# Two transformer half-layers on one Trainium2 core: the last two pairs of gate and up go to down's places without DRAM, the modulation sums are spread over the stages, one input combination moves to Pool

## The chip, the cores and the metric

The kernel runs on one core of a Trainium2 chip. The metric is the device time in microseconds of one execution; the time before is the median of three executions. Engines are named as in the profile: PE (matmul), DVE (vector), ACT (scalar), POOL (GpSimd), SP (the engine whose queue issues nearly all DMAs here).

## The reference

A hybrid decoder layer on x of 1024 tokens by 1024 columns, all float32, cut to what matters here:

```python
mod = (silu(c) @ w_ada + b_ada).reshape(9, 1024)          # nine modulation vectors
h = rms_norm(x, norm_ffn1) * (1 + mod[1]) + mod[0]
x = x + 0.5 * mod[2] * ((silu(h @ ffn1_gate) * (h @ ffn1_up)) @ ffn1_down)   # D_FF = 2816
h = rms_norm(x, norm_mix) * (1 + mod[4]) + mod[3]
...                                                        # projections, gated DeltaNet heads, pooling heads
x = x + mod[5] * (mixed @ w_out)
h = rms_norm(x, norm_ffn2) * (1 + mod[7]) + mod[6]
x = x + 0.5 * mod[8] * ((silu(h @ ffn2_gate) * (h @ ffn2_up)) @ ffn2_down)
return rms_norm(x, final_norm)
```

## The kernel before

**Precision.** Every float32 operand is split into a high part (ACT copy to fp32r) and a low part (DVE: value minus high part), and a product of a 128x128 weight block with a 128x512 activation tile is three matmuls of 512 columns: high by high, high by low, low by high.

**The two FFNs.** D_FF is cut into 22 columns of 128, in 11 pairs. Each of the two halves (`st` 0 and 1, for ffn1 and ffn2) computes one pair of gate and up directly, and the other ten as 2x2 block products with seven multiplications instead of eight (`SLOTS`: p1, p2, p5, p6, p3, p7, q4). Each slot needs a weight block or a sum of weight blocks, split into high and low (`split_weights`), and an input or a combination of inputs, also split (`combine_task`, `combo_split`). The combinations are made before the first pair of seven, from the four normed quarters `XN`. The seven products of a weight pair are added up while they are read out of PSUM (`gate_read`, `up_read`), and `parts_task` makes from the four results of a pair the seven parts that the down product takes as input, some by subtractions on POOL. Then ten of the pairs go through down in sevens again (`seven`, kind "d": thirteen products of 1, 2, 3, 4, 4, ... pairs of depth), and the last pair directly (`last_pair`).

**Ring.** The split parts of all pairs are written to DRAM (`part_task`, tensors gd) and come back into four places (pair modulo 4) of the tiles H, G, U and zs (`ring_task`, tiles H<-gd, G<-gd). These places are the very tiles that hold the inputs of gate and up, so for the first four pairs each of the seven kinds becomes free only with its last use in the last gate/up pair (flag `vfree`); for later pairs, when down has used the pair four before (`gfree`). The sums of down are added onto the residual rows, which come back from DRAM too (`rest_task`, A<-xpark in the first half, A<-rest in the second); they take their tiles from the sixteen A tiles that gate and up use as temporaries.

**Modulation vectors.** Two of the nine (scale and shift of the first norm) are made at the start. The other seven are made by `ada_tasks`, in fourteen chunks of 512 columns: eight DMAs of 256 KB into `ad` tiles, eight DVE instructions that add the weighted rows, four PE transposes into an `aux` bank, a DVE reduction.

**Order.** A planner (class `Order`) runs generators with assumed durations (`yield ("V", 0.6)` and so on: V is DVE, S is ACT, G is POOL, D is the DMA queue) and ranks, and the instructions of PE, DVE and ACT stay in the order in which it emits them. So an instruction whose input is late holds all that stand behind it on its engine. All DMAs of this part are issued on SP's one queue, in order as well; an SP instruction whose tile is not free holds the rest.

Of the kernel before, what the change touches and what calls it, by code (L numbers as in the profile page):

```python
# [11 lines left out]
ALU = mybir.AluOpType  # L12
# [12 lines left out]
NS = NPAIR - 1  # L25

# [110 lines left out]
def hybrid_layer_kernel(  # L137
# [367 lines left out]
    def w0_loads(u):  # L505
        return {(f, m): unit_load(w.rearrange("a (k p) f -> p (a k) f", p=P)[:, 4 * u : 4 * u + 4, f * P : (f + 1) * P]) for f, m, w in first}
# [117 lines left out]
    up1 = wunit(wsrc(ffn1_up, 1)[0])  # L624
# [80 lines left out]
    def ada_load(j, ch, k, cell):  # L705
        yield ("D", 0.5)
# [14 lines left out]
    def ada_tasks():  # L721
# [3 lines left out]
        for j, ch in seq:  # L725
            for k in range(KT):
                yield flag("ad", j, ch, k)
                raw, acc = cells[j, ch, k][0], cells[j, ch]
                yield ("V", 0.66 if k else 0.4)
# [50 lines left out]
    for st in range(2):  # L780
        wg, wu, wd = gates[st]
        todo = []
        for j in range(1, NPAIR):
# [33 lines left out]
    def seven_raws(st):  # L817
        for n, e in enumerate(plans[st]):
            tag = "cv" if n % 2 else "raw"
            for b in ("11", "21", "22", "12"):  # L820
                yield need(tag)
                yield ("D", 0.5)
# [7 lines left out]
    def seven_splits(st):  # L830
        for n, v in slots:
            yield need("split")
            spawn(split_weights(st, n, v), 1 if n < 2 else 3)

    def split_weights(st, n, v):
        nk = plans[st][n]["nk"]
        tt, cp = 0.08 + 0.13 * nk, 0.1 + 0.105 * nk
# [86 lines left out]
    def gate_read(st, n, v, ps, banks):  # L924
        j = plans[st][n]["j"]
        key = {"p2": (0, 0), "p3": (0, 1), "q4": (1, 0), "p7": (1, 1)}
        if v in ("p1", "p5", "p6"):
            yield need("tmp")
            yield ("S", 0.52)
# [4 lines left out]
        if v == "q4":  # L934
            yield need("tmp")
            yield ("S", 0.52, "Silu")
# [3 lines left out]
        else:  # L940
# [3 lines left out]
            yield ("V", 0.6)  # L944
# [5 lines left out]
            yield ("S", 0.52, "Silu")  # L950
# [4 lines left out]
    def up_read(st, n, v, ps, banks):  # L955
        j = plans[st][n]["j"]
        key = {"p2": (0, 0), "p3": (0, 1), "q4": (1, 0), "p7": (1, 1)}
        if v in ("p1", "p5", "p6"):
            yield need("tmp")
            yield ("S", 0.52)  # L960
# [4 lines left out]
        if v == "q4":  # L965
            yield flag("silu", st, j, key[v])
            i, t = made["s", st, j, key[v]]
            yield ("V", 0.6)
            V.tensor_tensor(t, t, ps, op=ALU.mult)
            put("mm")  # L970
        else:
# [3 lines left out]
            yield ("V", 0.6)  # L975
# [7 lines left out]
            yield ("V", 0.6)  # L983
# [5 lines left out]
    def down_read(st, n, v, ps, banks):  # L989
# [5 lines left out]
        yield ("V", 0.66)  # L995
# [11 lines left out]
    def silu_task(st, j, f, h, ps, tag):  # L1007
        yield need("tmp")
        yield ("S", 0.52, "Silu")
# [5 lines left out]
    def glu_task(st, j, f, h, ps, tag):  # L1015
        yield flag("silu", st, j, (f, h))
        yield ("V", 0.6)
# [8 lines left out]
    def first_rest():  # L1026
# [9 lines left out]
        spawn(glu_task(0, 0, 1, 1, ps, "mm"), 0.8)  # L1036

    def combine_task(st):
# [9 lines left out]
        for i, v in enumerate(("p5", "p7", "p6", "q4")):  # L1048
            for k in range(KT // 2):
                xa, xb, xc, xd = XN[k, 0], XN[k, 1], XN[k + 4, 0], XN[k + 4, 1]  # L1050
                b = shift[:, k + 4 : k + 5]
                yield ("V", 0.62)
                if i == 0:
                    V.tensor_tensor(xa, xb, xa, op=ALU.subtract)
                elif i == 1:
                    V.scalar_tensor_tensor(xb, xd, db[:, k : k + 1], xb, op0=ALU.add, op1=ALU.subtract)
                elif i == 2:
                    V.scalar_tensor_tensor(xd, xd, b, xa, op0=ALU.add, op1=ALU.subtract)
                else:
# [960 lines left out]
```

## Time and profile before

| | us |
|---|---|
| median of three runs | 1903.33 (1902.78 to 1908.27) |
| the profiled execution | 1904.2 |
| its span, first to last instruction | 1902.4 |
| PE busy in the span | 1806.9 |
| DVE busy in the span | 1395.1 |
| ACT busy, POOL busy | 773.3, 281.2 |

The profiled execution is 0.9 us over the median and has 1.8 us outside its span. Busy time of PE counts a matmul at either clock level as busy, so a stage can be busy and still slower than another. By stage: start and first products to about 97 us; gate and up of ffn1 to 529; down of ffn1 to about 735; projections, heads and output to about 1251; ffn2 the same again to about 1830; the last pair and the final norm to the end.

### The profile page before, as it was taken

What the parts mean: (1) busy time and instruction counts of PE and PEld (TensorE: products, weight loads), DVE (VectorE), ACT (ScalarE), POOL (GpSimd) and SP (SyncE); (2) the same over time, 40 slices, a digit from 0 to 9 for tenths busy, and PEclk for the clock granted to TensorE, in tenths of its full rate; (3) what the DMA queues carried; (4) which work ended last, traced back from release to release, by engine and by line L of the source; (5) the groups of instructions that cost most, each with busy time, mean ns of one, the idle gap of its engine ahead of it and who ended that gap; (6) DMA issues with size and microseconds to landing.
All of it is one profiled execution on the core that took longest, in us unless ns stands there. A gap on an engine that the chain in (4) does not pass through costs nothing.

```text
span 1902.4 us, 24995 instructions
## 1 busy us (share of the span) xinstructions
PE 1806.9 (95%) x8437; PEld 1483.4 (78%) x8437; DVE 1395.1 (73%) x2450; ACT 773.3 (41%) x1527; POOL 281.2 (15%) x229
## 2 busy tenths in 40 slices
PE   7899898999979999999999999999999999979997
PEld 6677776788858887788888878878888888758876
DVE  4899999886666667878787674696667666756676
ACT  5453333344422223464344253354444444312225
POOL 3421111111100003121121012211211121000004
PEclk9889999999989999999999999999999999989998
DMA  9447777755698754122121135415345535997722
GB/s 329 160 128 244 237 232 227 235 192 181 231 348 275 248 176 140 45 63 49 34 48 47 46 124 154 122 62 193 122 137 180 170 122 166 330 331 257 232 79 89
DMA packets 311008, 322.66 MB, mean 170 GB/s; under 512 B 28437, under 2 KB 215890, under 8 KB 310880
## 3 DMA queue, kind: packets, MB, share of 16 engines
q1 hardware_dynamic: 310304, 319.93, 52.3%
q8 instruction: 67, 1.10, 0.2%
q0 software_dynamic: 576, 1.13, 0.2%
q14 instruction: 61, 0.50, 0.1%
HBM read 223.21 MB, written 97.78 MB: 169 GB/s over the span
## 4 chain that ended last, share of the span: by engine, by line
PE 76%; DVE 11%; DMA 7%; issue 3%; ACT 1%; POOL 1%; SPq 0%; ACTq 0%; POOLq 0%; DVEq 0%
PE mm L155 44%; PE po L155 24%; PE aux L155 7%; DVE A L155 3%; DVE ad L155 2%; DVE split L155 2%; PE rec L155 2%; DVE pm L155 1%; DMA ad<-in_w_ada 1%; DMA gd<-A 1%; DMA adah<-in_w_ada 1%; DMA G<-gd 1%; DVE G L155 1%; DMA H<-gd 1%; DMA raw<-in_ffn_gate 1%
## 5 line engine op out<-in xcount | busy, mean ns | idle before, releaser
L155 PE MATMUL mm<-H,split 128*128 128x512 f32 (+1 forms) x3096 | 770.2, 396 | 8.8 <-DVE A L155 7.2
L155 PEld LDWEIGHTS mm<-H,split 128*128 128x128 f32 x3096 | 571.3, 190 | 126.7 <-DVE A L155 7.4
L155 PE MATMUL po<-H,split 128*128 128x512 f32 x1584 | 390.1, 395 | 32.4 <-DVE A L155 25.8
L155 PEld LDWEIGHTS po<-H,split 128*128 128x128 f32 x1584 | 298.8, 190 | 99.9 <-issue 28.3
L155 PE MATMUL mm<-G,split 128*128 128x512 f32 x1440 | 348.9, 394 | 2.5 <-DVE G L155 1.8
L155 PEld LDWEIGHTS mm<-G,split 128*128 128x128 f32 x1440 | 272.6, 190 | 62.6 <-DVE G L155 3.2
L155 ACT CAST split<-pm 128x512 fp32r<-128x512 f32 (+3 forms) x264 | 152.8, 581 | 352.7 <-DVE pm L155 351.5
L155 DVE TENSOR_TENSOR split<-pm,split 128x512 fp32r<-128x512 f32 (+3 forms) x264 | 185.0, 704 | 108.7 <-ACT split L155 105.5
L155 POOL TENSOR_TENSOR A<-A,A 128x512 f32<-128x512 f32 x80 | 125.2, 1574 | 666.7 <-DVE A L155 420.4
L155 ACT CAST split<-raw 128x512 fp32r<-128x512 f32 (+2 forms) x199 | 117.2, 595 | 187.2 <-PE mm L155 107.8
L155 PE MATMUL po<-U,split 128*128 128x512 f32 x480 | 156.7, 392 | 4.1 <-DVE A L155 4.1
L155 DVE TENSOR_TENSOR split<-raw,split 128x512 fp32r<-128x512 f32 (+2 forms) x199 | 133.2, 679 | 19.2 <-ACT split L155 18.9
L155 DVE SCALAR_TENSOR_TENSOR A<-mm,fg,A 128x512 f32<-128x512 f32 (+1 forms) x144 | 103.1, 718 | 54.9 <-PE mm L155 36.8
L155 DVE TENSOR_TENSOR A<-A,A 128x512 fp32r<-128x512 f32 (+1 forms) x208 | 141.1, 691 | 2.2 <-ACT A L155 2.2
L155 PEld LDWEIGHTS po<-U,split 128*128 128x128 f32 x480 | 90.7, 189 | 24.1 <-ACT A L155 2.6
L155 POOL TENSOR_TENSOR acc<-acc,cv 128x512 f32<-128x512 f32 (+1 forms) x46 | 56.6, 1229 | 345.0 <-ACT cv L155 343.9
L155 DVE SCALAR_TENSOR_TENSOR A<-po,fg,A 128x512 f32<-128x512 f32 x78 | 58.1, 749 | 53.9 <-PE po L155 44.0
L155 PE MATMUL po<-zs,split 128*128 128x512 f32 x240 | 94.1, 392 | 0.0
L155 ACT CAST split<-cv 128x512 fp32r<-128x512 f32 (+1 forms) x96 | 57.0, 594 | 90.8 <-PE po L155 52.2
L155 DVE SCALAR_TENSOR_TENSOR ad<-ad,cs,ad 128x512 f32<-128x512 f32 x98 | 84.5, 863 | 11.9 <-DMA ad<-in_w_ada 10.8
L155 ACT CAST A<-A 128x512 fp32r<-128x512 f32 x148 | 88.5, 619 | 10.3 <-DVE A L155 8.4
L155 DVE TENSOR_TENSOR split<-cv,split 128x512 fp32r<-128x512 f32 (+1 forms) x96 | 64.1, 668 | 21.9 <-ACT split L155 21.4
(270 smaller groups left out, 1821.1 us busy)
## 6 DMA issues: line engine op xcount, KB each, us to landing
gd<-A SPq DMA_DIRECT2D x296, 256.0 KB, 3.9
H<-gd SPq DMA_DIRECT2D x88, 512.0 KB, 4.6
ad<-in_w_ada SPq DMA_DIRECT2D x112, 256.0 KB, 3.3
raw<-in_ffn_gate SPq DMA_DIRECT2D x88, 256.0 KB, 3.8
cv<-in_ffn_up SPq DMA_DIRECT2D x80, 256.0 KB, 4.5
G<-gd SPq DMA_DIRECT2D x80, 256.0 KB, 3.7
raw<-in_w_in SPq DMA_DIRECT2D x40, 256.0 KB, 2.9
adah<-in_w_ada SPq DMA_DIRECT2D x32, 256.0 KB, 5.9
```

What stands on the lines that cost most here:

```text
L155: ins = f(*args, **kwargs)
```

## The change

- The direct pair is now pair 1 (`PAIR0`), and the ten others come in the order 3 to 10, then 0, then 2 (`PAIRS`). The last two (`DIRECT`) skip `part_task` and DRAM: `direct_task` writes high and low part right into the place that down reads, when `vfree` of the slot has come. Pairs 1 and 3, the other two of the first four places, are read back from DRAM, and their writes have been issued long before. `ring_task` and `rest_task` become `feed_task` and `rest_load`.
- The fourteen chunks of the modulation vectors start at flags (`start`): those of mod 2, 4 and 3 from the weights of the third pair of ffn1 on, mod 5 and 7 in down of ffn1, mod 6 in the projections, mod 8 in ffn2. In the built program six of the fourteen stand ahead of down of ffn1, four in it, two in the projections, two in ffn2; before, all fourteen stood ahead of down of ffn1.
- Of the four combinations of the inputs, the third (p7) is a POOL subtraction without the shift (`combine_third`); the shift goes into the high and low part.
- H tiles are loaded from DRAM by two DMAs of 256 KB instead of one of 512 KB, and the planner's assumed durations are larger (DVE 0.6 to 0.7, a DMA 0.5 to 0.78, and so on).

```diff
+PAIR0 = 1
+PAIRS = (3, 4, 5, 6, 7, 8, 9, 10, 0, 2)
+DIRECT = PAIRS[-2:]
...
     def ada_loads(seq, cells):
+        start = {(2, 0): ("W", 0, 4, "p1"), (5, 0): ("gfree", 0, 0, "q4"), (6, 0): ("H", 1, KT - 1, 1), (8, 0): ("W", 1, 4, "p1")}
         for j, ch in seq:
+            if (j, ch) in start:
+                yield flag(*start[j, ch])
             yield need("ad")
...
-        for j in range(1, NPAIR):
+        for j in PAIRS:
...
-        for i, v in enumerate(("p5", "p7", "p6", "q4")):
...
+        for k in range(KT // 2):
+            yield ("V", 0.72)
+            V.tensor_tensor(XN[k, 0], XN[k, 1], XN[k, 0], op=ALU.subtract)
+            spawn(combo_split(st, k, "p5", XN[k, 0]), 1.4)
+            spawn(combine_third(st, k, db[:, k : k + 1]), 1.5)
...
+    def combine_third(st, k, b):
+        yield ("G", 1.3)
+        G.tensor_tensor(XN[k, 1], XN[k + 4, 1], XN[k, 1], op=ALU.subtract)
+        mark(("t3", st, k))
+        spawn(combo_split(st, k, "p7", XN[k, 1], b), 1.4)
...
         for v, src in todo:
+            if j in DIRECT:
+                spawn(direct_task(st, j, v, *src), 1.6 if j == DIRECT[0] else 2.8)
+                continue
...
+    def direct_task(st, j, v, i, src):
+
+        yield flag("vfree", st, v)
+        yield ("S", 0.62)
+        mv = ring[st, j, v] = place_of(v, j)
+        S.copy(mv[0], src)
+        yield ("V", 0.7)
+        V.tensor_tensor(mv[1], src, mv[0].bitcast(F32), op=ALU.subtract)
+        release(i)
+        mark(("G", st, j, v))
...
-    def ring_task(st):
+    def feed_task(st):
 
         for p in range(NPAIR):
             r = p % 4
+            if p < 4:
+                for d in (2 * p, 2 * p + 1):
+                    for h in range(2):
+                        spawn(rest_load(st, d, h), 2.5)
+            if p in DIRECT:
+                continue
             for v in SLOTS if p < NS else ((0, 0), (0, 1), (1, 0), (1, 1)):
```

**DVE in the third of the ten pairs of ffn1.** The order on DVE of the kernel before, around its reads of the slots p7 (ad is a sum of a modulation chunk, split and pm are weights, an A on both sides is a product being read out or a part):

```order
L155 SCALAR_TENSOR_TENSOR ad_427_1929<-ad_462_2082,cs_157,ad_427_1929 128x512
L155 TENSOR_TENSOR A13_432_1949<-A13_432_1949,mm_394_1794 128x512
L155 SCALAR_TENSOR_TENSOR ad_427_1929<-ad_464_2093,cs_157,ad_427_1929 128x512
L155 TENSOR_TENSOR split_469_2128<-raw_451_2037,split_469_2128 128x512
L155 SCALAR_TENSOR_TENSOR ad_427_1929<-ad_465_2097,cs_157,ad_427_1929 128x512
L155 TENSOR_TENSOR A12_440_1980<-A12_440_1980,mm_400_1820 128x512
L155 SCALAR_TENSOR_TENSOR ad_427_1929<-ad_466_2106,cs_157,ad_427_1929 128x512
L155 TENSOR_TENSOR A12_440_1980<-A12_440_1980,A13_432_1949 128x512
L155 TENSOR_TENSOR split_472_2151<-cv_463_2086,split_472_2151 128x512
L155 SCALAR_TENSOR_TENSOR ad_427_1929<-ad_468_2115,cs_157,ad_427_1929 128x512
```

The changed kernel around the same two reads (the helper's line is 160 there):

```order
L160 TENSOR_TENSOR split_434_2011<-cv_428_1979,split_434_2011 128x512
L160 TENSOR_TENSOR A9_405_1869<-A9_405_1869,mm_370_1721 128x512
L160 TENSOR_TENSOR split_436_2027<-raw_425_1963,split_436_2027 128x512
L160 SCALAR_TENSOR_TENSOR ad_371_1726<-ad_419_1931,cs_157,ad_371_1726 128x512
L160 TENSOR_TENSOR A14_412_1898<-A14_412_1898,mm_375_1744 128x512
L160 SCALAR_TENSOR_TENSOR ad_371_1726<-ad_423_1953,cs_157,ad_371_1726 128x512
L160 TENSOR_TENSOR A14_412_1898<-A14_412_1898,A9_405_1869 128x512
L160 TENSOR_TENSOR split_439_2052<-cv_435_2022,split_439_2052 128x512
L160 TENSOR_TENSOR pm_443_2075<-raw_408_1879,raw_411_1896 128x512
L160 SCALAR_TENSOR_TENSOR ad_371_1726<-ad_437_2036,cs_157,ad_371_1726 128x512
```

The sums of modulation chunks stand thinner: of their 112 first-step and adding instructions 3 stood in the first of the ten pairs, 18 to 20 in each of the second to sixth, 13 in the seventh; now 4 stand in the second pair, 12, 13 and 12 in the next three, 7 in the sixth.

**SP where gate and up of ffn1 end.** The queue before, some way into the loads behind the last gate/up product (H, G, U and zs are places of the ring, gd on the left a part that is written out, A<-xpark a residual row):

```order
L1127 DMA gd_1071_4997<-A8_1023_4827 128x512
L1154 DMA H2_1_1073_5010<-gd_452_2040 128x1024
L1127 DMA gd_1071_4997<-A14_989_4669 128x512
L1154 DMA H3_0_1075_5021<-gd_507_2307 128x1024
L1171 DMA A1_1078_5027<-xpark_180_811 128x512
L1154 DMA H7_0_1081_5037<-gd_510_2316 128x1024
L825 DMA raw_1083_5044<-in_ffn1_down 128x4x128
L1149 DMA U_1085_5050<-gd_516_2346 128x512
L1151 DMA zs_1086_5051<-gd_516_2346 128x512
L1171 DMA A14_1090_5065<-xpark_177_805 128x512
L1149 DMA G6_1092_5073<-gd_520_2361 128x512
L1171 DMA A8_1094_5076<-xpark_181_813 128x512
```

The changed kernel, from the load for slot p1 of pairs 1 and 3 on:

```order
L1197 DMA H1_0_848_4197<-gd_239_1088 128x512 x2
L1197 DMA H3_0_921_4523<-gd_319_1461 128x512 x2
L1197 DMA H5_0_863_4254<-gd_261_1176 128x512
L833 DMA raw_865_4263<-in_ffn1_down 128x128
L1197 DMA H5_0_863_4254<-gd_261_1176 128x512
L1197 DMA H7_0_924_4537<-gd_322_1471 128x512 x2
L1208 DMA A7_867_4278<-xpark_134_593 128x512
L1197 DMA zs_878_4312<-gd_269_1206 128x512
L833 DMA raw_872_4297<-in_ffn1_down 128x128
L833 DMA raw_874_4303<-in_ffn1_down 128x128
L1197 DMA U_877_4311<-gd_269_1206 128x512
L833 DMA cv_890_4366<-in_ffn1_down 128x2x128
```

Before, the loads of three whole pairs, the writes of the last parts and the residual rows stand behind the last gate/up product in one queue; now the loads of pairs 1 and 3 go side by side from slot p1 on, no write stands between them, and pairs 0 and 2 are not in the queue.

**DVE in the third of down's products.** The rows of the kernel before around the first read of the third product (mm_1068, columns 4 and 5):

```order
L155 TENSOR_TENSOR A14_989_4669<-A14_989_4669,A8_1023_4827 128x512
L155 SCALAR_TENSOR_TENSOR A11_1005_4753<-mm_1035_4871,fg0_173,A11_1005_4753 128x512
L155 TENSOR_TENSOR split_1072_4999<-pm_1067_4988,split_1072_4999 128x384
L155 TENSOR_TENSOR pm_1074_5014<-pm_1067_4988,raw_1014_4796 128x384
L155 SCALAR_TENSOR_TENSOR A15_1011_4780<-mm_1068_4990,fg0_173,A15_1011_4780 128x512
L155 TENSOR_TENSOR pm_1079_5031<-raw_1036_4875,pm_1074_5014 128x384
L155 TENSOR_TENSOR split_1076_5023<-pm_1074_5014,split_1076_5023 128x384
```

The changed kernel around the same read (mm_968):

```order
L160 TENSOR_TENSOR split_972_4701<-pm_971_4698,split_972_4701 128x384
L160 TENSOR_TENSOR H2_0_939_4579<-A9_854_4205,H2_0_939_4579 128x512
L160 TENSOR_TENSOR split_974_4706<-pm_973_4703,split_974_4706 128x384
L160 TENSOR_TENSOR H6_0_941_4590<-A6_910_4480,H6_0_941_4590 128x512
L160 TENSOR_TENSOR zs_943_4597<-A13_918_4514,U_942_4596 128x512
L160 SCALAR_TENSOR_TENSOR A0_936_4573<-mm_968_4685,fg0_173,A0_936_4573 128x512
L160 SCALAR_TENSOR_TENSOR A15_905_4461<-mm_933_4567,fg0_173,A15_905_4461 128x512
```

The low parts of pair 2 (H2_0, H6_0, zs) now stand right ahead of that read, which needs the first of them; 33 instructions stand from the first read of down to this one before, 39 now.

## Rows read from the trace of the kernel before

**Rows 1.** The page, busy time by engine: busy us (share of the span) xinstructions.

```profile
PE 1806.9 (95%) x8437; PEld 1483.4 (78%) x8437; DVE 1395.1 (73%) x2450; ACT 773.3 (41%) x1527; POOL 281.2 (15%) x229
```

**Rows 2.** Windows: stretch, its us, busy by engine, clock, DMA share, GB/s.

```profile
96.70:529.20 432.50, 405.04 (x1737) 328.67 (x1736) 372.98 (x569) 183.02 (x324) 65.39 (x39) 0.96 0.66 214
404.00:529.00 125.00, 124.74 (x553) 103.40 (x554) 84.42 (x133) 54.81 (x98) 17.29 (x12) 1.00 0.57 190
529.20:593.60 64.40, 51.34 (x212) 40.23 (x211) 42.82 (x76) 15.83 (x32) 0.00 (x0) 0.89 0.97 333
593.60:735.00 141.40, 141.14 (x622) 116.30 (x620) 91.76 (x151) 31.42 (x58) 1.21 (x2) 1.00 0.60 191
```

**Rows 3.** Timeline of PE, ffn1's gate and up: start us, us, instructions.

```profile
91.22 11.04 PE L155 MATMUL mm<-H,split 128*128 128x512 f32 x48
...
139.06 8.32 PE L155 MATMUL mm<-H,split 128*128 128x512 f32 x36
...
485.69 11.04 PE L155 MATMUL mm<-H,split 128*128 128x512 f32 x48
...
523.77 6.28 PE L155 MATMUL mm<-H,split 128*128 128x512 f32 x27
```

**Rows 4.** Waits of PE in 160:400: us in total, times, longest.

```profile
PE aux L155 <- DVE ad L155: 15.1, 7, 4.2
```

**Rows 5.** Timeline of PE around transposes of modulation chunks.

```profile
176.12 0.66 PE L155 MATMUL aux<-ident,ad 128*128 128x128 f32 x4
176.53 5.26 PE L155 MATMUL mm<-G,split 128*128 128x512 f32 x22
...
271.83 3.33 PE L155 MATMUL mm<-G,split 128*128 128x512 f32 x7
```

**Rows 6.** Groups of instructions, DVE in 160:400: busy us, mean ns.

```profile
L155 DVE SCALAR_TENSOR_TENSOR ad<-ad,cs,ad 128x512 f32<-128x512 f32 x89 | 76.8, 863 | 11.0 <-DMA ad<-in_w_ada 10.1
L155 DVE TENSOR_REDUCE red<-aux 128x4 f32<-128x512 f32 x12 | 8.2, 685 | 1.2 <-PE aux L155 1.1
```

**Rows 7.** Timeline of DVE in the first of the ten pairs.

```profile
103.77 1.78 DVE L155 SCALAR_TENSOR_TENSOR A<-G,db,A 128x512 f32<-128x512 f32 x1
...
120.58 0.74 DVE L155 SCALAR_TENSOR_TENSOR G<-G,mod,ad 128x512 f32<-128x512 f32 x1
121.24 0.68 DVE L155 TENSOR_TENSOR G<-G,G 128x512 fp32r<-128x512 f32 x1
121.85 0.74 DVE L155 SCALAR_TENSOR_TENSOR G<-G,mod,G 128x512 f32<-128x512 f32 x1
```

**Rows 8.** Timeline of POOL, the subtractions of the first parts.

```profile
97.95 10.43 POOL L155 TENSOR_TENSOR A<-A,A 128x512 f32<-128x512 f32 x3 [4.29 <-issue]
```

**Rows 9.** Timeline of PE in both down stages.

```profile
566.40 4.18 PE L155 MATMUL po<-H,split 128*128 128x512 f32 x9 [12.54 <-DVE A L155]
570.38 2.27 PE L155 MATMUL mm<-G,split 128*128 128x512 f32 x9
...
590.85 5.60 PE L155 MATMUL mm<-H,split 128*128 128x512 f32 x24
...
1682.51 4.18 PE L155 MATMUL po<-H,split 128*128 128x512 f32 x9 [12.61 <-DVE A L155]
```

**Rows 10.** The chain that ended last, 538:566: start us, us, what.

```profile
552.03 7.19 DMA H<-gd
...
559.24 6.25 DMA A<-xpark
...
565.51 0.76 DVE A L155
```

**Rows 11.** Timeline of DVE, first reads of down's first and third product.

```profile
530.22 0.75 DVE L155 SCALAR_TENSOR_TENSOR A<-mm,fg,A 128x512 f32<-128x512 f32 x1
...
545.02 0.75 DVE L155 SCALAR_TENSOR_TENSOR A<-mm,fg,A 128x512 f32<-128x512 f32 x1
```

**Rows 12.** Waits of SP's queue in 160:400.

```profile
SPq L708 <- DVE ad L155: 85.8, 61, 5.0
```

More of the change, by code (lines that the diff above doesn't have):

```diff
@@ L705, in ada_load @@
     def ada_load(j, ch, k, cell):
-        yield ("D", 0.5)
+        yield ("D", 0.78)
         cell.append(ad())
@@ L1081, in combo_split @@
             mv = gtile(8 + 2 * k, F32R), gtile(9 + 2 * k, F32R)
-        S.copy(mv[0], src)
-        yield ("V", 0.6)
-        V.tensor_tensor(mv[1], src, mv[0].bitcast(F32), op=ALU.subtract)
+        if v == "p7":
+            S.activation(mv[0], src, AF.Identity, bias=b)
+            yield ("V", 0.77)
+            V.scalar_tensor_tensor(mv[1], src, b, mv[0].bitcast(F32), op0=ALU.add, op1=ALU.subtract)
+        else:
+            S.copy(mv[0], src)
+            yield ("V", 0.7)
+            V.tensor_tensor(mv[1], src, mv[0].bitcast(F32), op=ALU.subtract)
         if v == "p7":
@@ L1144, in ring_task, with rest_load @@
                 yield flag("gd", st, p, v)
-                yield ("D", 0.5)
-                src = gdram[st, p, v]
-                if place in ("p5", "p6", "p7"):
-                    mv = (utile(F32R), ztile(F32R)) if place == "p5" else tuple(gtile((0 if place == "p6" else 8) + 2 * r + e, F32R) for e in range(2))
-                    nc.sync.dma_start(out=mv[0].bitcast(F32), in_=src[:, 0])
-                    yield ("D", 0.5)
-                    nc.sync.dma_start(out=mv[1].bitcast(F32), in_=src[:, 1])
-                else:
-                    ht = htile(r + (4 if place in ("p2", "p3") else 0), 1 if place in ("p3", "q4") else 0)
-                    nc.sync.dma_start(out=ht.bitcast(F32), in_=src)
-                    mv = ht[:, 0], ht[:, 1]
-                key = (st, p, v) if p < NS else (st, p, *v)
-                ring[key] = mv
-                spawn(arrive(("G", *key), 3.0), 3)
-    def rest_task(st):
-        yield flag("vfree", st, "p1")
-        for t in range(4):
-            for d in (2 * t, 2 * t + 1):
-                for h in range(2):
-                    while ("cut", st) not in order.flags and len(free) < 5:
-                        yield ("wait", 0.5)
-                    yield need("tmp")
-                    A[d, h] = temp()[1]
-                    yield ("D", 0.5)
-                    nc.sync.dma_start(out=A[d, h], in_=rest[st][d, h])
-                    spawn(arrive(("rest", st, (d, h))), 3)
+                key = (st, p, v) if p < NS else (st, p, *v)
+                for e in range(2):
+                    yield ("D", 0.78)
+                    if e == 0:
+                        ring[key] = place_of(place, r)
+                    nc.sync.dma_start(out=ring[key][e].bitcast(F32), in_=gdram[st, p, v][:, e])
+                spawn(arrive(("G", *key)), 3)
+    def rest_load(st, d, h):
+        yield flag("vfree", st, "p1")
+        while ("cut", st) not in order.flags and len(free) < 5:
+            yield ("wait", 0.5)
+        yield need("tmp")
+        A[d, h] = temp()[1]
+        yield ("D", 0.78)
+        nc.sync.dma_start(out=A[d, h], in_=rest[st][d, h])
+        spawn(arrive(("rest", st, (d, h))), 3)
     def last_src(wd, dp):
```

112 lines of the change are left out of this document (58 added, 54 removed).

## The prediction

> **What bounds the kernel now.** I read busy times first, then windows by stage, then PE's timeline and waits inside the stages in which it loses time. PE is busy 1806.9 of 1902.4 us [rows 1], so at most about 95 us of idle time can be won, and beyond that only what PE does at the lower clock. Two places hold most of both.
>
> The first is gate and up of ffn1. Its ten pairs run from 96.66 (the second half of the 48 matmuls at 91.22, 24 matmuls of 0.2267 us later) to 529.21 (24 matmuls after 523.77), 432.5 us [rows 3]. One undisturbed pair is 168 matmuls in 523.77 - 485.69 = 38.08 us [rows 3], so 0.2267 us each, and ten are 380.8. The stage loses 51.7 us: 432.5 - 405.0 = 27.5 idle [rows 2], fourteen groups of transposes of modulation chunks at 0.41 us (176.53 - 176.12) [rows 5], 5.7, and the rest, 18.5, at the lower of the two clock levels. After one such wait a row of seven matmuls spans 3.33 us, about 0.45 us each with their overlap, where they take 0.2267 otherwise [rows 5]. The largest wait of this stretch is PE's for the DVE sum of a modulation chunk, 15.1 us from 160 to 400 [rows 4]. DVE is the cause: busy 373.0 of 432.5 us, and more densely in the first 307 us, since from 404 on, with no chunk left, it is busy only 84.4 of 125 [rows 2].
>
> The second is the start of down in both halves. There PE waits 12.54 and 12.61 us in one piece [rows 9]. The chain leads back from DVE's read over the residual row's load (6.25 us), which stood in the one queue behind ring loads (7.19 us) [rows 10]; the DMA engines are full, share 0.97 at 333 GB/s [rows 2]. The first four products of down are 210 matmuls, 47.6 us; they end at 593.57 (24 matmuls after 590.85, less the 12 of the next product), that is 64.4 after 529.21 [rows 9]. The place costs 16.8 us, and I take the second half's for the same.
>
> **Spreading the modulation sums.** A chunk costs DVE eight instructions at 0.66 us and a reduction of 0.69, together 6.0 us; the pitch is that of scalar_tensor_tensor, 121.24 - 120.58 [rows 6, 7]. A pair without chunks holds 39 tensor_tensor at a pitch of 0.61 (121.85 - 121.24) [rows 7], 23.8 us, and is measured at 84.42/125 x 38.08 = 25.7 [rows 2]; the difference is DVE's time beside POOL. With 18 to 20 chunk instructions per pair, 2.4 chunks, a pair of before needs 25.7 + 14.4 = 40.1 us of DVE against 38.08 of PE: DVE cannot keep up, so PE waits, falls to the lower clock, and goes on. With 12 or 13 it is 1.6 chunks, 35.3 us, 93% of the pair. That fits, but closely: an instruction order in which a late one holds all others will still cost something. I take 1.2 us of stall in each of the five pairs with chunks (0 to 4 as bounds, the upper being what the longest wait for a chunk cost [rows 4]) and the six transposes, 2.5: 8.5 us lost, 0.5 in the pair without.
>
> **The first pair and POOL's combination.** The first of the ten pairs ends at 144.5 (24 matmuls after 139.06) and so takes 47.8 us, 9.8 too many [rows 3]. Of DVE's work for it, the four scalar_tensor_tensor that move to POOL go, 2.7 us at 0.66, and the three chunk instructions, up to 2 us. What POOL costs DVE is bounded by one row: a DVE instruction took 1.78 us instead of 0.74 while POOL worked [rows 7], so four times 1.04, 4.2 us, at most, and nothing where DVE is idle or reads PSUM; POOL's own three took 10.43 us there, 3.5 each, so the fourth of the new ones may be late for the p6 combination [rows 8]. I take a net gain of 2 us (bounds: a loss of 2, a gain of 4), 7.8 us still lost. The Trainium skill speaks against this move: its page "SBUF — State Buffer", section "SBUF: two separate sides", says that a DVE instruction with two SBUF inputs and a GpSimd one share a port pair as an exclusive lock, and that the second waits for the whole of the first. By that rule the four POOL subtractions would take as much from DVE as they give, and the sum would be about 2 us worse; the 1.78 us row agrees with a wait, and the 10.43 us row with waits on POOL's side.
>
> Together gate and up of ffn1 lose 7.8 + 0.5 + 8.5 = 16.8 in place of 51.7: **-34.9**.
>
> **Pairs 0 and 2 without DRAM.** What ended PE's wait was a residual row behind ring loads. Now two of four pairs' loads (7.3 MB of 14.7) and their writes are out of the queue, the other two start with slot p1, six of the last pair's seven slots before the end (32.6 us), and the first residual rows stand ahead of them. So the long wait goes. What is late next is DVE: between down's first read and the first read of the third product 33 instructions took 545.02 - 530.22 = 14.8 us [rows 11], back to back; now 39 stand there, 14.8 x 39/33 = 17.5, since pair 2's low parts are due now and those of pairs 9 and 10 were not. The third product's first matmuls are due 14.3 us after the start, so PE waits some 3 us for H2_0, and the rest of that product runs at DVE's pace. I take 5 us of the 16.8 as still lost (1 to 12 as bounds): **-11.8 in each half, -23.6**. The two DMAs for one H tile move the same bytes.
>
> **What the moved chunks cost where they go.** Eight groups of transposes, 3.3 us, on a PE that is busy all the time there. Down of ffn1 takes four chunks within about 84 us: 24 us of DVE, which is busy 91.8 of 141.4 there, and 8.4 MB, 25 us at 333 GB/s, on DMA engines at a share of 0.60 [rows 2]. Both fit; the loads stand among ring loads. I take 0.4 us of waiting at each of the eight places, 3, and 2 us for late ring loads (0 to 12 together): **+8.3**. The changed assumptions of the planner reorder the stage between; I take nothing, plus or minus 4.
>
> **Sum.** -34.9 - 23.6 + 8.3 = -50.2. The profiled execution of 1904.2 becomes 1854.0, and its 0.9 us over the median taken off, 1853.
>
> **The rivals.**
> *The modulation work only moves.* Its price is paid in down: if DVE or the queue were full there, the 24 or 25 us would come back and the kernel take about 1877. For it: ring loads have to come within one product's 19 us, on the same queue. Against: the shares of 0.65 and 0.60 above. 0.07.
> *A new wait at the start of down.* Pairs 0 and 2 hold their temporaries until slots are free, residual rows need tiles from the same sixteen; if the residual rows or H2_0 come as late as before, 23.6 us stay and the time is 1877. 0.07.
> *More than I give it.* If with DVE relieved all stalls go but transposes and half of the first pair's, and down starts with 1 us lost: 10 us more, then 8: about 1835. 0.06.
> *Slower than before: SP's queue in down.* A chunk's load waits for its buffer and holds all behind it: 61 such waits, 1.4 us each, at most 5.0 [rows 12]. Then 32 of these stand between ring loads. If each held the queue with nothing running ahead, a mean of 1.4 us would add 45 us to 84 us of stage; 50 us of gain are used up from a mean of about (50 + 43)/32 = 2.9 us on, where 43 us are what the queue has to spare (half of the stage). At 5.0 each, 160 us: about 1970. Against: the wait is for DVE, which has room there. 0.03.
> The case of the sum: 0.77, 1837 to 1874.
>
> **How the numbers follow.** The prediction is the first sum. Its terms' bounds, taken together and not all at one end, are about 20 us to either side; 1834 to 1876 leaves out the slower rival and the two at 1877, 0.17, and what of the better one lies below. Less than 0.3% (5.7 us) is what a measurement of this kernel can tell from no change. All cases but the last end far below: faster 0.95, same 0.02, slower 0.03.
>
> **What would show it.** Right: PE's wait for DVE ad from 160 to 400 under 5 us; the ten pairs of ffn1 in 391 to 406 us; no wait over 5 us where down begins, and the residual rows' DMA out of the chain; PE still at the full clock in down of ffn1. Wrong: DVE at 9 tenths or more in down of ffn1 with waits for zs, H or G loads; the 12.5 us wait again; a POOL subtraction in the chain near 115 us.

## The result, and the profile after

The changed kernel takes 1860.39 us (median of four runs, 1859.98 to 1863.49) beside 1903.05 (1902.0 to 1908.27) for the kernel before: a ratio of 0.977, 95% interval 0.975 to 0.980, 42.7 us less. The prediction was 1853 with a range of 1834 to 1876.

The page's busy times of the changed kernel, beside [rows 1]:

```profile
PE 1794.3 (97%) x8437; PEld 1474.6 (79%) x8437; DVE 1401.7 (75%) x2442; ACT 773.1 (42%) x1527; POOL 300.6 (16%) x237
```

Its span is 1858.2 us, so PE's idle time fell from 95.5 to 63.9 us, and its busy time by 12.6 us for the same matmuls, since fewer of them run at the lower clock (the mean granted clock of the span is 0.991 in place of 0.977).

The windows of the changed kernel for gate and up of ffn1, the first four products of down and the rest of down, with the columns of [rows 2]:

```profile
96.30:493.30 397.00, 388.84 (x1706) 317.97 (x1705) 320.17 (x479) 181.89 (x322) 63.26 (x39) 1.00 0.56 183
493.30:547.20 53.90, 48.83 (x211) 38.98 (x210) 45.65 (x79) 17.32 (x35) 1.26 (x1) 1.00 0.62 187
547.20:687.00 139.80, 139.54 (x624) 115.27 (x623) 111.28 (x183) 30.70 (x56) 1.21 (x2) 1.00 0.77 256
```

Gate and up: 397.0 in place of 432.5 us, with 90 DVE instructions fewer, a clock of 1.00 in place of 0.96. The start of down: 53.9 in place of 64.4, with the DMA engines at 0.62 in place of 0.97. Behind it DVE and the DMA engines have more to do than before (111.28 for 91.76 us, 0.77 for 0.60): the moved chunks.

PE's timeline at the places of [rows 3] and [rows 9], then at the start of ffn2:

```profile
90.82 11.04 PE L160 MATMUL mm<-H,split 128*128 128x512 f32 x48
...
112.43 0.79 PE L160 MATMUL po<-zs,split 128*128 128x512 f32 x1 [2.73 <-DVE zs L160]
...
138.65 11.04 PE L160 MATMUL mm<-H,split 128*128 128x512 f32 x48
...
487.82 6.28 PE L160 MATMUL mm<-H,split 128*128 128x512 f32 x27
...
499.66 0.96 PE L160 MATMUL mm<-G,split 128*128 128x512 f32 x3 [2.17 <-ACT split L160]
500.46 2.31 PE L160 MATMUL mm<-H,split 128*128 128x512 f32 x9
...
513.22 2.11 PE L160 MATMUL mm<-H,split 128*128 128x512 f32 x8 [2.01 <-DVE H L160]
...
544.48 5.60 PE L160 MATMUL mm<-H,split 128*128 128x512 f32 x24
...
1215.22 17.66 PE L160 MATMUL mm<-H,split 128*128 128x512 f32 x70 [3.33 <-DVE split L160]
...
1605.94 6.28 PE L160 MATMUL mm<-H,split 128*128 128x512 f32 x27
...
1617.78 1.65 PE L160 MATMUL mm<-G,split 128*128 128x512 f32 x3 [2.17 <-ACT split L160]
1619.22 3.13 PE L160 MATMUL mm<-H,split 128*128 128x512 f32 x9
...
1632.79 2.11 PE L160 MATMUL mm<-H,split 128*128 128x512 f32 x8 [2.01 <-DVE H L160]
...
1664.09 5.60 PE L160 MATMUL mm<-H,split 128*128 128x512 f32 x24
```

Read as in the prediction: the ten pairs run from 96.26 to 493.26 (24 matmuls, 5.44 us, after each row's start), the first of them to 144.09, the first four products of down to 547.20 (12 matmuls, 2.72 us, after 544.48). In the second half down starts at 1611.38 and its first four products end at 1666.81, 55.4 us; before they took from 1645.23 to 1709.69, 64.5. No wait over 2.2 us is left at either start of down, and H2_0's low part is late by 2.01 us in both, where 3 was forecast. The second start takes 1.5 us more than the first with the same waits (2.17 and 2.01 us the longest). The twelve matmuls behind the wait of 2.17 us make the difference: 2.95 us from 499.66 on, at a granted clock of 1.00, and 4.41 us from 1617.78 on, at 0.62. What decides the level that PE has behind such a wait is not shown by these traces.

PE's waits from 160 to 400 us in the changed kernel, in place of the row in [rows 4]:

```profile
PE aux L160 <- DVE ad L160: 2.3, 3, 1.0
```

So by position: 35.5 us won in gate and up of ffn1, 10.5 at the first start of down, 9.0 at the second; of the lead of 46.4 us at 547 only 33.85 are left where down of ffn2 starts, 12.5 given back; 0.4 come ahead of gate and up and 1.3 at the end. That sums to the 44.2 us between the two spans.

### The profile page after: what moved, and what is told of

The parts are those of the page before. It is cut to its first block, busy times and chain, and to the rows that moved or that the text cites. A ratio compares the mean times of both kernels' runs of the same rounds, so it can differ in the third digit from the quotient of the medians.

```text
span 1858.2 us, 24957 instructions
## 1 busy us (share of the span) xinstructions
PE 1794.3 (97%) x8437; PEld 1474.6 (79%) x8437; DVE 1401.7 (75%) x2442; ACT 773.1 (42%) x1527; POOL 300.6 (16%) x237
## 4 chain that ended last, share of the span: by engine, by line
PE 83%; DVE 10%; issue 3%; DMA 2%; ACT 1%; POOL 1%; SPq 0%; ACTq 0%; POOLq 0%; DVEq 0%
PE mm L160 47%; PE po L160 27%; PE aux L160 6%; DVE A L160 2%; PE rec L160 2%; DVE split L160 2%; DVE pm L160 2%; DVE G L160 1%; DMA adah<-in_w_ada 1%; DVE ad L160 1%; DVE cv L160 1%; DVE H L160 1%; DMA raw<-in_ffn_down 0%; DMA xpark<-A 0%; ACT A L160 0%
## 5 line engine op out<-in xcount | busy, mean ns | idle before, releaser
L160 PE MATMUL mm<-G,split 128*128 128x512 f32 x1440 | 344.7, 390 | 7.3 <-ACT split L160 4.3
L160 POOL TENSOR_TENSOR A<-A,A 128x512 f32<-128x512 f32 x80 | 129.1, 1625 | 678.9 <-DVE A L160 392.7
L160 DVE TENSOR_TENSOR split<-pm,split 128x512 fp32r<-128x512 f32 (+3 forms) x264 | 175.5, 672 | 56.7 <-ACT split L160 56.1
L160 DVE SCALAR_TENSOR_TENSOR A<-mm,fg,A 128x512 f32<-128x512 f32 (+1 forms) x144 | 103.0, 719 | 65.5 <-PE mm L160 64.5
L160 DVE TENSOR_TENSOR split<-raw,split 128x512 fp32r<-128x512 f32 (+2 forms) x199 | 133.3, 679 | 23.4 <-ACT split L160 23.0
L160 DVE TENSOR_TENSOR A<-A,A 128x512 fp32r<-128x512 f32 (+1 forms) x180 | 122.2, 686 | 3.1 <-ACT A L160 0.6
L160 DVE TENSOR_TENSOR A<-A,po 128x512 f32<-128x512 f32 x86 | 58.9, 685 | 43.4 <-PE po L160 43.0
L160 ACT CAST A<-A 128x512 fp32r<-128x512 f32 x120 | 72.9, 620 | 40.1 <-DVE A L160 38.6
```

Source lines behind the costliest of these rows:

```text
L160: ins = f(*args, **kwargs)
```

## The experiments

The theory that the prediction stands on: the chunks of modulation vectors were too dense in ffn1's gate and up, and **moving eight of fourteen elsewhere** makes room; the direct pairs take the waits at the starts of down. The rivals: the new assumed durations alone do it, the residual rows' place in the queue does it, POOL helps or hurts.

All runs, with the three stages read from PE's timeline as above. The stages are those of the profiled execution, which need not be the median one (e7 1848.99, e10 1849.07, e11 1852.58, e9 1854.9). The intervals are of the ratio to runs of the kernel before taken beside each; their medians lay from 1903.05 to 1906.88 us, so 2 or 3 us between two rows do not tell two kernels apart where their intervals overlap.

| kernel | median us | ratio, 95% | gate and up of ffn1 | first four of down 1 | of down 2 |
|---|---|---|---|---|---|
| before | 1903.05 | 1 | 432.5 | 64.4 | 64.5 |
| the change | 1860.39 | 0.975 to 0.980 | 397.0 | 53.9 | 55.4 |
| e1, new planner numbers only | 1893.89 | 0.992 to 0.995 | 409.3 | 72.2 | 71.7 |
| e2, change without start flags | 1860.26 | 0.974 to 0.978 | 402.8 | 55.4 | 55.5 |
| e3, change without direct pairs | 1877.47 | 0.983 to 0.986 | 399.3 | 63.0 | 63.2 |
| e4, change, third combination on DVE | 1862.37 | 0.975 to 0.978 | 398.6 | 57.0 | 55.1 |
| e5, before, one number | 1874.04 | 0.983 to 0.986 | 401.6 | 65.3 | 64.9 |
| e6, change with slack | 1857.87 | 0.974 to 0.977 | 396.2 | 55.4 | 55.4 |
| e7, e2 with slack, units first | 1853.07 | 0.972 to 0.975 | 398.5 | 58.5 | 53.9 |
| e8, before, one number and direct pairs | 1854.45 | 0.972 to 0.975 | 400.0 | 55.7 | 55.7 |
| e9, e8 with slack, units first | 1852.72 | 0.971 to 0.974 | 397.7 | 60.9 | 55.7 |
| e10, e7, third combination on DVE | 1853.09 | 0.971 to 0.974 | 398.3 | 58.4 | 53.9 |
| e11, e7, slower pace | 1848.75 | 0.969 to 0.973 | 395.3 | 57.4 | 58.3 |
| e12, e1 with the old DMA numbers | 1897.71 | 0.995 to 0.997 | 405.5 | 75.5 | 72.7 |

**e1: the planner's numbers alone.** The kernel before, with all new assumed durations and ranks:

```diff
-                yield ("V", 0.66 if k else 0.4)
+                yield ("V", 0.78 if k else 0.5)
...
-            yield ("V", 0.6)
+            yield ("V", 0.7)
...
-            yield ("D", 0.5)
+            yield ("D", 0.78)
```

> The kernel before with the planner's new assumed durations and ranks alone; no piece of work is moved, and H tiles are still loaded by one DMA. Theory (the moves made the gain): the time stays within about 4 us of 1903, that is 1899 to 1907; PE still waits over 10 us in one piece at both starts of down, and ffn1's gate and up still take about 430 us. Rival (the truer assumptions made the planner place the same work better): 1875 or less, with ffn1's gate and up under 410 us.

Measured: 1893.89, between the two. Windows of this run, gate and up and the two starts of down:

```profile
95.00:504.30 409.30, 393.11 (x1737) 320.44 (x1737) 376.13 (x570) 184.14 (x325) 63.90 (x39) 0.99 0.70 225
504.30:576.50 72.20, 55.00 (x211) 41.51 (x210) 43.52 (x75) 16.09 (x32) 0.00 (x0) 0.91 0.89 308
1628.30:1700.00 71.70, 54.86 (x211) 41.03 (x211) 43.60 (x75) 15.99 (x32) 0.00 (x0) 0.90 0.89 305
```

Neither theory had this: 23 us are won in gate and up with every chunk still inside it (570 DVE instructions, as the 569 before), and 8 and 7 are lost at the starts of down.

**e2: no start flags.** The changed kernel with all fourteen chunks as early as their buffers allow:

```diff
-        start = {(2, 0): ("W", 0, 4, "p1"), (5, 0): ("gfree", 0, 0, "q4"), (6, 0): ("H", 1, KT - 1, 1), (8, 0): ("W", 1, 4, "p1")}
+        start = {}
```

> The changed kernel without the flags at which the chunks of the modulation vectors start, so that all fourteen run as early as their buffers let them. Theory: DVE again has more than a pair's 38.08 us in each pair with 2.4 chunks, so ffn1's gate and up take about 425 to 432 us in place of 397.0, while the eight moved chunks no longer cost what they cost later (8 to 13 us): 1860 + 28 to 35 - 8 to 13, that is 1876 to 1887. Rival (the new assumed durations already keep the chunks out of the way, and the flags only move the cost): 1860 to 1866.

Measured: 1860.26, no difference. Its windows of gate and up and of the start of down:

```profile
96.60:499.40 402.80, 394.34 (x1737) 320.93 (x1736) 371.64 (x562) 183.46 (x323) 63.68 (x39) 0.99 0.69 222
499.40:554.80 55.40, 50.33 (x212) 40.22 (x211) 45.78 (x79) 17.44 (x35) 1.26 (x1) 0.97 0.59 181
```

The theory falls. With fourteen chunks in the stage it takes 5.8 us more than with six, not 30; and its lead of 38.8 us after the start of down shrinks only to 34.1 by the second down, 4.7 in place of 12.5. The moved chunks cost 7.8 us where they go, and save 7.3 where they were (5.8 in the stage, 1.5 at the start of down). What thinned the chunks was not that some left, but how fast the planner sets them: from the first to the last of the fourteen groups of transposes in PE's timeline it is 248.5 us in the kernel before (155.8 to 404.3), 19.1 from one to the next; here 320.1 (164.1 to 484.2), 24.6.

**e5: that pace alone.** The kernel before with one number changed, the assumed time of a chunk's DVE instruction:

```diff
-                yield ("V", 0.66 if k else 0.4)
+                yield ("V", 1.1 if k else 0.8)
```

> The kernel before with one number changed: the planner takes a DVE instruction of a modulation chunk for 1.1 us in place of 0.66, and so plans about 1.5 chunks in a pair of ffn1's gate and up in place of 2.4; all fourteen still stand ahead of down. Theory (the pace at which the planner lets the chunks into DVE's order is what the gain of gate and up hangs on): the second to tenth of the ten pairs lose 14 to 20 us in place of 42, the starts of down stay at 64 us each, and the time is 1876 to 1883. Rival (what helped was the truer duration of all other DVE work, which moves reads and splits): 1893 or more, with PE's waits for DVE ad still over 12 us.

Measured: 1874.04, ratio 0.983 to 0.986, 30 us by a number that no instruction contains, and 2 us below what the theory gave. Windows as for e1, and PE's wait from 160 to 400:

```profile
96.40:498.00 401.60, 393.02 (x1738) 321.74 (x1737) 375.64 (x569) 183.58 (x325) 65.43 (x39) 0.99 0.71 229
498.00:563.20 65.20, 50.75 (x211) 39.70 (x210) 42.64 (x76) 15.81 (x32) 0.00 (x0) 0.92 0.98 338
1614.50:1679.40 64.90, 50.83 (x212) 39.74 (x211) 42.89 (x76) 15.89 (x32) 0.00 (x0) 0.89 0.99 342
```

```profile
PE aux L155 <- DVE ad L155: 2.5, 4, 0.8
```

The same 569 DVE instructions with the same busy time (375.64 and 372.98 us) lie in a stage that is 31 us shorter. The second to tenth pair lose 10.9 us in place of 42 (the theory had 14 to 20). From the first to the last of the chunks' transposes it is 319 us, 24.5 each. The planner's sum shows why: it fills with chunks what it believes DVE has left in a pair. At 39 instructions of 0.60 that is 38.08 - 23.4 = 14.7 us, and a chunk taken for 0.4 + 7 x 0.66 + 0.8 = 5.8 goes in 2.5 times; taken for 9.3, 1.6 times; and with the change's 0.70 and 0.78, 10.8 us over 6.8, 1.6 times again. DVE needs 25.7 us for a pair and 6.0 for a chunk [rows 2, 6, 7]: 1.6 fit into 38.08, 2.5 do not. The starts of down stay as they were (65.3 and 64.9 us, DMA engines at 0.98 and 0.99), so the gain is kept to the end. e1, with a like pace, loses 15 us at the starts of down; e12 below asks which of its numbers does it.

**e3: no direct pairs.** The changed kernel, all pairs through DRAM in their old order:

```diff
-PAIR0 = 1
-PAIRS = (3, 4, 5, 6, 7, 8, 9, 10, 0, 2)
-DIRECT = PAIRS[-2:]
+PAIR0 = 0
+PAIRS = tuple(range(1, NPAIR))
+DIRECT = ()
...
-        if j == DIRECT[-1]:
-            mark(("cut", st))
...
+            if v == (1, 1):
+                mark(("cut", st))
```

The flag `cut`, from which on residual rows take any free tile, stands behind the last pair's parts again, as in the kernel before.

> The changed kernel with pairs 1 to 10 in their old order and none direct: all parts go through DRAM again, the direct first pair is pair 0; spread chunks, the POOL combination, two DMAs for an H tile and the residual rows' early place in the queue stay. Theory: the last pairs' writes and all four pairs' loads are back in the queue where down begins, so both starts of down lose 15 to 17 us again in place of 6.3 and about 8: 1860 + 16 to 21, that is 1876 to 1881. Rival (the residual rows' place ahead of the ring loads is what removed the wait): 1860 to 1866, and no wait over 4 us at either start of down.

Measured: 1877.47, 17 us more than the change, as the theory had it. The chain that ended last, in this run where down begins:

```profile
507.18 0.69 DVE A L160
...
507.89 0.34 SPq L1168
...
508.28 0.67 SPq L1197
...
509.00 1.16 SPq L1208
...
510.20 0.43 SPq L1197
...
510.68 5.38 DMA A<-xpark
...
516.14 0.76 DVE A L160
...
517.04 2.90 PE po L160 x6
```

PE waits 10.45 us there again and 11.17 in the second half, for DVE's read, which waits for the residual row's load (L1208, `rest_load`) that stands among ring loads (L1197). As in [rows 10] the row comes last; here the chain leads back to the write of a part (L1168), which came behind DVE's work on an A tile (the row at 507.18). The stages say the same: 63.0 and 63.2 us in place of 53.9 and 55.4. So the direct pairs as a whole are worth 17 us. The rows' place was not held fixed, though: in e3 six of the sixteen rows' loads are issued before down begins, in the change nine. Against the rival speaks the kernel before, which issues nine ahead as well and still waits 12.54 us. How much of the 17 us is fewer transfers in the queue, and how much that parts which are not written hold fewer of the tiles that rows need, was not separated.

**e4: the third combination back on DVE.**

```diff
-        yield ("G", 1.3)
-        G.tensor_tensor(XN[k, 1], XN[k + 4, 1], XN[k, 1], op=ALU.subtract)
+        yield ("V", 0.72)
+        V.tensor_tensor(XN[k, 1], XN[k + 4, 1], XN[k, 1], op=ALU.subtract)
```

> The changed kernel with the four subtractions of the third combination on DVE in place of POOL, in both halves; everything else the same. The term of the prediction (POOL saves DVE 2 us net in the first pair): 2 us slower in each half, 1863 to 1865. Theory after the result (the first pair still loses 9.75 us as before, so the move bought nothing): within 1.5 us of 1860.4. Rival (POOL's subtractions make DVE wait as long as they save, and the p6 combination waits for them): 2 to 4 us faster in each half, 1852 to 1857.

Measured: 1862.37, between the two forecasts, and the intervals of e4 and the change overlap. The first pair takes 49.4 us (94.52 to 143.96, 24 matmuls after the rows at 89.08 and 138.52) in place of 47.8, but PE's waits in it are nearly the same, 5.9 us in place of 5.7; 14 matmuls behind one of them take 4.94 us (from 121.92 on, clock 0.64) where the change's take 3.31 (from 123.14 on, clock 1.00). At the first start of down (57.0 in place of 53.9), where no combination is made, PE has the waits of the change (0.42, 2.17, 2.02 and 0.46 us), and slower matmuls behind them. The windows of those behind the wait for H2_0, in e4 and in the change:

```profile
514.62:518.10 3.48, 3.48 (x9) 2.77 (x9) 2.28 (x4) 0.62 (x1) 0.00 (x0) 0.52 0.82 231
```

```profile
513.22:515.17 1.95, 1.95 (x8) 1.60 (x9) 1.95 (x4) 0.62 (x1) 0.00 (x0) 1.00 0.79 176
```

So neither place shows a price or a gain of the move itself. The trace shows what POOL costs at the other place, the start of ffn2. POOL and DVE there in the changed kernel:

```profile
1198.63 9.73 POOL L160 TENSOR_TENSOR A<-G,A 128x512 f32<-128x512 f32 x4 [15.06 <-issue]
```

```profile
1202.66 1.15 DVE L160 TENSOR_TENSOR split<-raw,split 128x512 fp32r<-128x512 f32 x1 [0.55 <-ACT split L160]
1203.74 1.77 DVE L160 SCALAR_TENSOR_TENSOR G<-G,mod,ad 128x512 f32<-128x512 f32 x1
1205.44 1.78 DVE L160 TENSOR_TENSOR zs<-ad,U 128x512 fp32r<-128x512 f32 x1
1207.14 1.77 DVE L160 SCALAR_TENSOR_TENSOR G<-G,mod,ad 128x512 f32<-128x512 f32 x1
1208.83 0.68 DVE L160 TENSOR_TENSOR G<-G,G 128x512 fp32r<-128x512 f32 x1
```

and DVE at the same place of e4:

```profile
1205.74 0.69 DVE L160 TENSOR_TENSOR split<-raw,split 128x512 fp32r<-128x512 f32 x1 [0.55 <-ACT split L160]
...
1206.95 0.69 DVE L160 TENSOR_TENSOR zs<-ad,U 128x512 fp32r<-128x512 f32 x1
1207.55 0.75 DVE L160 SCALAR_TENSOR_TENSOR G<-G,mod,ad 128x512 f32<-128x512 f32 x1
```

Beside POOL four DVE instructions take 6.47 us in place of 0.69 + 0.75 + 0.69 + 0.75 = 2.88, 3.6 more; the four subtractions on DVE would have taken 4 x 0.69 = 2.8. The move saves nothing here. The page "SBUF — State Buffer" of the Trainium skill, section "SBUF: two separate sides", has the two engines shut each other out at a shared port pair; these rows agree with that. Its cost in time hardly shows, since DVE's order then decides what PE waits for: PE's wait at this place is 3.33 us with POOL and 2.73 in e4.

**e6 and e7: slack, and the weights first.** In the changed kernel, 3 us between a chunk's last sum and its transposes in the planner's reckoning; in e7 no start flags, and the last weight splits of ffn2's direct pair ranked ahead of the combinations too:

```diff
+            yield ("wait", 3.0)
             yield need("aux")
             yield ("PE", 0.43)
...
-            spawn(unit_split(key), 3)
+            spawn(unit_split(key), 1 if key in (len(units) - 2, len(units) - 1) else 3)
```

> The changed kernel with 3 us more, in the planner's reckoning, between the last sum of a modulation chunk on DVE and its transposes on PE, so that the transposes stand later in PE's order. Theory (each moved chunk costs about 1 us because PE waits for a sum that is a little late and then works at the lower clock for a while): PE's waits for DVE ad, 3.8 us in five, go, with them part of the half-clock rows: 3 to 8 us faster than 1860.4, that is 1852 to 1857. Rival (the wait only goes to the next instruction that DVE is late for): 1859 to 1862.

Measured: 1857.87, 2.5 us less than the change, just outside what the theory gave (1852 to 1857) and under the rival's; the intervals of the two overlap. PE no longer waits for a chunk's sum in gate and up; the second to tenth pair lose 3.3 us in place of 6.4, about the six groups of transposes. Elsewhere 3.8 us are lost again: the first pair takes 50.1 us in place of 47.8 (14 matmuls from 121.03 on at a clock of 0.65), the first start of down 55.4 in place of 53.9; and the stage begins 2.8 us earlier (93.47 in place of 96.26). So the 2.5 us do not tell what the slack is worth by itself.

> The changed kernel without the start flags (all chunks in ffn1's gate and up again, as in the earlier run), with the 3 us of slack ahead of the transposes, and with the last two weight splits of ffn2's direct pair ranked ahead of the input combinations. Theory: gate and up of ffn1 take about 397 to 400 us in place of 402.8 without slack, PE's wait of 3.33 us for a split at ffn2's start goes with 1.6 us at the lower clock behind it, nothing is paid in the stages between: 1850 to 1855. Rival (what isn't waited for there is waited for in the first pair of ffn2, where the combinations come later): 1856 to 1861.

Measured: 1853.07, as the theory had it, with gate and up at 398.5 us. PE's timeline of e7 at ffn2's start has 72 matmuls without a wait, where the change has 3.33 us:

```profile
1209.70 16.48 PE L160 MATMUL mm<-H,split 128*128 128x512 f32 x72
```

**e8 to e11: how little is needed.** e8 is the kernel before with e5's one number and the direct pairs (order of pairs, `direct_task`, `place_of`, `feed_task` with its two DMAs for an H tile, `rest_load`); no flag, no other number, no POOL. e9 adds the two edits of e6 and e7 to it. e10 is e7 with e4's edit. e11 is e7 with

```diff
-                yield ("V", 0.78 if k else 0.5)
+                yield ("V", 1.0 if k else 0.7)
```

> The kernel before with two pieces: the one number for the pace of the chunks (1.1 in place of 0.66), and the pairs' order with the two direct pairs, their places and the feed of ring and residual rows. All other planner numbers are the old ones, no start flags, all four combinations on DVE as before. Theory (these two carry the whole gain, pace 30 and direct pairs 17 us, and the rest of the change brings nothing): 1854 to 1859, no slower than the whole change's 1860.4. Rival (the direct pairs need the truer numbers for DMA and DVE, or the chunks' end near down takes their gain): 1863 or more.

Measured: 1854.45 (1853.92 to 1854.73), as the theory had it and 6 us less than the whole change, the intervals apart. Its gate and up:

```profile
95.60:495.60 400.00, 392.46 (x1738) 321.71 (x1737) 370.92 (x566) 182.46 (x322) 66.96 (x38) 0.99 0.69 223
```

Here the stage has all fourteen chunks and takes 3 us more than in the change; but of the lead of 42.3 us after the first start of down, 40.4 are left at the second (1604.79, 24 matmuls after the row at 1599.35), so 1.8 is given back in place of 12.5.

> The kernel of the run with pace and direct pairs only, with the 3 us of slack ahead of the chunks' transposes and ffn2's last two direct splits ranked ahead of the combinations. Theory: slack is worth 3 us in gate and up of ffn1 as it was in the changed kernel, the ranks bring nothing here since PE does not wait for a split there with the old order of combinations: 2 to 4 us faster than that run. Rival: no difference, within 1.5 us.

Measured: 1852.72 (1850.68 to 1854.9), 1.7 less than e8: between theory and rival, not settled.

> The run without flags, with slack and the units first (1853), with the third combination on DVE in place of POOL. Theory (POOL and DVE cost each other what the move saves; the earlier trial of this edit was 2 us slower for reasons of order in down): within 2 us of 1853. Rival (DVE beside POOL takes 1.77 us for instructions of 0.7 at ffn2's start, so that DVE alone is faster there): 1847 to 1850.

Measured: 1853.09, the same as e7 to 0.02 us: where POOL's four subtractions are done makes no difference that can be measured.

> The run without flags, with slack and the units first (1853), with a chunk instruction taken for 1.0 us in place of 0.78, so that about 1.15 chunks fall into a pair and the last three into down of ffn1. Theory (once DVE keeps up, a chunk costs PE about what its transposes take, wherever it stands): within 2 us of 1853. Rival (fewer chunks in a pair still relieve it): 1846 to 1850.

Measured: 1848.75 (1847.54 to 1852.58), 4 us less than e7 (1848.99 to 1854.15), the fastest kernel of the study. It speaks for the rival, but the runs of the two overlap. In e7, e9, e10 and e11 the first start of down takes 57.4 to 60.9 us, more than the 53.9 of the change; why is not shown.

**e12: what e1 loses at the starts of down.** e1 with the assumed durations of the DMAs as before:

```diff
-            yield ("D", 0.78)
+            yield ("D", 0.5)
```

> The first run (the kernel before with the new planner numbers alone) with the assumed durations of the DMAs set back to the old ones, so that only the numbers for DVE, ACT and POOL and the ranks are new. Theory (the larger numbers for DMAs set the ring's loads and residual rows later and cost the 15 us at the two starts of down): the pace of the chunks stays at about 1.5 in a pair, the starts of down fall from 72 to about 65 us each, and the time is 1874 to 1880. Rival (the larger numbers for DVE and ACT at the starts of down cost it): 1888 or more, with the starts of down still at about 72 us.

Measured: 1897.71, the rival. The pace stays (gate and up 405.5 us), and the starts of down take 75.5 and 72.7 us. The new ranks are in it as well. PE's timeline there, in both halves:

```profile
548.41 4.18 PE L155 MATMUL po<-H,split 128*128 128x512 f32 x9 [22.25 <-DVE A L155]
...
1675.43 4.18 PE L155 MATMUL po<-H,split 128*128 128x512 f32 x9 [20.27 <-DVE A L155]
```

The waits of [rows 9], 12.5 us there, are 22.25 and 20.27 with larger numbers for DVE, ACT and POOL. The chain that ends the first of them runs over a part's write (4.59 us) and then the residual row's load (4.17 us), where that of [rows 10] has a ring load ahead of the row. With direct pairs the same numbers do no such harm: the change's starts of down take 53.9 and 55.4 us, those of e8 with the old numbers 55.7.

## Why the prediction was right, and where its steps failed

**The sum was right by 7 us, one of its reasons was not.** Gate and up of ffn1 won 35.5 us where 34.9 stood, and lost 16.2 where 16.8 stood; that this is so close is partly chance, since the first pair loses 2 us more than forecast and the nine others 2.6 less (6.4 in place of 9.0). The starts of down won 4.1 us less than forecast, and what was given back between is 4.2 us more. The account of DVE behind it (40.1 us for a pair with 2.4 chunks, 35.3 with 1.6) is borne out by e5 and e2. But one step failed: that the spreading makes the chunks thinner. The new durations were counted only in "The changed assumptions of the planner reorder the stage between; I take nothing, plus or minus 4"; the thinner chunks were read in the changed order, where six stand in the stage, and put down to the flags. In e2 the flags are worth 0; in e5 one assumed duration, on the kernel before, is worth 30 us. It could have been worked out ahead: the sum of 14.7 us over 5.8 needs only the code and the 38.08 of a pair.

**The first pair.** Forecast 7.8 us lost, measured 9.75, as before (9.8). The term "a net gain of 2 us" for POOL is not seen: PE's waits in this pair are 5.7 us, 5.9 in e4, and e10 is no slower than e7. Its bounds (-2 to +4) held. DVE's time beside POOL was in them; that the price eats the gain was not taken as the likely case, though the longer DVE row was there [rows 7].

**The starts of down.** Forecast -23.6, measured -10.5 and -9.0, and e3 gives 9.1 and 7.8 back when the direct pairs are undone. The mechanism was right, the term mis-sized by 4: 6.3 and 7.8 us are still lost in place of 5. No load of a residual row stands in the chain of the change from 490 to 550. That "the first residual rows stand ahead" does not tell the two kernels apart: nine of the sixteen are issued before down begins in both. H2_0 was named and is late by 2.01; PE's wait of 2.17 us for ACT's split in the first product of down was not foreseen. DVE's rows, the first read of down and the first of the third product:

```profile
494.14 0.75 DVE L160 SCALAR_TENSOR_TENSOR A<-mm,fg,A 128x512 f32<-128x512 f32 x1
...
514.76 1.40 DVE L160 SCALAR_TENSOR_TENSOR A<-mm,fg,A 128x512 f32<-128x512 f32 x2
```

They lie 20.6 us apart, not 17.5; the wait for H2_0 was still under the forecast because PE itself came late to it, 18 us after the start in place of 14.3, so the nearness of 2.01 to 3 is chance.

**The moved chunks.** Forecast +8.3; the difference between the change and e2 is 12.5 - 4.7 = 7.8. Right in size; but it is the whole price of what the flags save. The other 4.7 lie just outside the "plus or minus 4": with e8, which keeps the old numbers, 1.8 are given back, so some 3 come from the new numbers, the combinations on POOL or the slower matmuls behind waits, which were not told apart. One piece is seen: the wait of 3.33 us at ffn2's start, which e7 takes away.

**The rivals.** "The modulation work only moves" was near for the flags alone: their gain and their price are both between 7 and 8 us. "A new wait at the start of down" and "SP's queue in down" did not come: no wait over 2.2 us stands there, and the rest of down, with four chunks in it, took 1.9 us longer than before (to the 6 matmuls at 686.89 in PE's timeline, which stood at 731.35). POOL's rule came out as an equal exchange.

What stays open: by which step the larger numbers for the engines lengthen the wait at the starts of down in e1 and e12, and at which clock level PE goes on behind a wait of some 2 us, which makes 1.5 to 3 us between like places (the two starts of down in the change, the first ones of e4 and the change).

## What to carry to other kernels

Where a planner with assumed durations writes a fixed order, work that fills gaps runs as densely as those durations say, so a duration that is a tenth too short can make a busy engine late in every round, and one larger number for the filler may give what moving the work would; try that before moving anything. Divide the time of a round by what the planner believes and by what the trace shows, and compare how much filler each lets in. A long wait where one stage follows another is to be looked for at its queue: here fewer transfers in it helped (53.9 us), where another order of all of them did little (63.0 in e3, 64.4 before). And before a microsecond or two at one place is put down to an edit, the waits and the clock behind them are to be compared: the same waits can cost 3 us more.

## What the runs showed of the hardware

Four DVE instructions of 128x512 beside POOL's subtractions took 1.15 to 1.78 us, where the like take 0.69 to 0.75 alone, and POOL's four took 9.73 us together, 2.4 each. DVE's instructions just ahead of these, in the same 9.73 us, are not all longer (three at 1199.61 take 1.89 us): the longer ones come in a run, not evenly. The mean granted clock of gate and up rose from 0.96 to 0.99 in e5 with the same matmuls and DVE instructions in another order: PE's waits for a chunk's sum fell from 15.1 us in seven [rows 4] to 2.5 in four between 160 and 400, and its busy time in the stage from 405.0 to 393.0 us. Behind like waits of 2.0 to 2.2 us PE went on at a granted clock of 1.00 (499.66 and 513.22 in the change) or at 0.52 and 0.62 (514.62 in e4, 1617.78 in the change), which made 1.5 us for eight or twelve matmuls each time.
